# Output projection beside the attention heads, divided anew by columns and tokens, with splits ordered behind evictions

## The chip, the cores and the metric

The kernel runs on one core of one Trainium2 chip. The metric is device microseconds of one execution of the whole layer; lower is better. Five engines work side by side: TensorE (PE in the profile; PEld are its weight loads), VectorE (DVE), ScalarE (ACT), GpSimd (POOL) and SyncE (SP), which issues nearly all DMAs here. Each engine runs its instructions in order and waits for the others through semaphores.

## The reference

One layer on x of 1024 tokens by 1024 features, with a memory of 256 tokens, all float32:

```python
h = h + parallel_mixer(rms_norm(h, norm_mix_g), w_in, ..., w_out)
h = h + memory_cross_attention(rms_norm(h, norm_xattn_g), rms_norm(mem, norm_mem_g), ...)
u = jax.nn.relu(rms_norm(h, norm_mlp_g) @ mlp_w1)
h = h + (u * u) @ mlp_w2
```

The mixer projects x, runs forgetting attention over 8 heads of width 64 (causal, softmax of `q.k / 8` plus a sum of log forget gates) and gated linear attention (GLA) over 4 heads, and multiplies both results, side by side, by `w_out`:

```python
return jnp.concatenate([fox_out, gla_out], axis=-1) @ w_out
```

So rows 0 to 511 of `w_out` meet the attention's output and rows 512 to 1023 that of the GLA. The cross attention has 4 heads of width 256 and takes its keys and values from `memn @ wkv`.

## The kernel before

**Products.** Every float32 operand is split into a high part of a shorter format and a low part (the rest), and `gemm` (line 103) makes three matmuls for each k-tile of 128: high by high, high by low, low by high (lines 108 to 110). A split is a copy on ScalarE and a subtraction on VectorE. For weights `wsplit` (line 67) does it: it loads two k-tiles of 128x512 in one DMA on SP into one of 2 `raw` buffers (line 78), copies each to `wh` on ScalarE (line 86) and subtracts to `wl` on GpSimd in two halves (line 89) or on VectorE (line 91). With `lo_pool=1` every tile is subtracted on GpSimd, with 2 every other one, with 0 none. There are 9 slots for `wh` and 9 for `wl`, taken in turn. For the mixer's outputs `split_half` (line 794) splits, for one half of the tokens (512), one k-tile after the other into buffers `sh` and `sl` (lines 802 and 803).

**The heads.** `fox` (line 645) runs 8 heads. A head has two groups of four score blocks and four blocks of values; after each of the 32 value blocks `step(s)` (line 687), s = 0 to 31, advances a generator of side work by one item or by none. Score blocks go from TensorE (`s`, lines 627 to 630) over a maximum on VectorE (632), an exponential on ScalarE (635) and a scaling on GpSimd (638); value blocks transpose p on TensorE (667), split it (115 and 116) and multiply (674 and 675). The result lands in `mixf` (line 680), k-tile h // 2 for head h, so the first two k-tiles of the attention are complete after head 3, the third after head 5. The GLA's output `mixg` is complete before the heads start.

**The side work** (`side_work`, line 704) has 26 items:

- `out_part(.., 0, ())`, items 1 to 8: columns 0 to 511 of the projection, GLA part only. The k-tiles of the GLA are 4, so an item, one block of 128 columns for one half of the tokens, is 4 x 3 = 12 matmuls. First four items for the first half of the tokens, then four for the second.
- items 9 and 10: the memory is loaded and split; the gains `gx` are made (lines 713 to 716).
- items 11 to 18: the keys and values of the memory, `wkv` in four column groups n of 8 k-tiles for two token tiles each: 24 matmuls an item. Results go into one buffer `mkv` and from there by DMA to DRAM (lines 738 and 752).
- `out_part(.., 1, range(2))`, items 19 to 26: columns 512 to 1023, 4 k-tiles of the GLA and 2 of the attention: 18 matmuls an item.

An item of `out_part` ends by adding the residual from x to the accumulator on VectorE (the eviction, line 776, tile `t2k`) and storing the sum in DRAM (`hpd`). The accumulators of the side work come from a pool with one bank (`mm2`, line 650), so the next item's first matmul waits for this one's eviction. Item 1 runs before head 0, and the pacing `(s * 30 + 8) // 32` makes item 26 fall to step 26.

**The projection behind the heads** (`project_out`, line 808) adds what is left: for columns 0 to 511 all four k-tiles of the attention, for columns 512 to 1023 the last two (`ks`, line 815), for both halves of the tokens, with six accumulator banks. It loads `hpd` (line 821), adds it (826), squares the result on ScalarE and adds the squares up on GpSimd (`add_squares`, line 159) for the norm of the cross attention, which follows with its query products.

**Order.** The program states the operations, but the order of instructions on each engine is made by a planner that simulates the whole program in time: an operation may be placed ahead of others of its engine that come earlier in the text, where buffers and data allow. `tc.issue_after(ins)` makes all instructions traced inside it follow `ins` on the engine of `ins`.

Of the kernel before, what the change touches and what calls it, by code (L numbers as in the profile page):

```python
# [22 lines left out]
ALU = mybir.AluOpType  # L23
# [28 lines left out]
class Layer:  # L52
# [59 lines left out]
    def evac_split(self, hi, lo, ps, scale=None):  # L112
        nc = self.nc
        if scale is None:
            nc.scalar.activation(hi, ps, AF.Copy)
            nc.vector.tensor_tensor(lo, ps, f(hi), ALU.subtract)
        else:
            nc.scalar.activation(hi, ps, AF.Identity, scale=scale)
            nc.vector.scalar_tensor_tensor(lo, ps, scale, f(hi), ALU.mult, ALU.subtract)
# [75 lines left out]
    def build(self):  # L195
        with ExitStack() as st:
# [13 lines left out]
            self.consts(self.open(st, "const"))  # L210
            self.smallp = self.open(st, "small", 6)
# [433 lines left out]
    def fox(self):  # L645
        nc = self.nc
        with ExitStack() as st:
# [39 lines left out]
            def step(s):  # L687
                for _ in range(((s + 1) * 30 + 8) // 32 - (s * 30 + 8) // 32):
                    next(side, None)
# [14 lines left out]
    def side_work(self, mp, mmp, trp):  # L704
# [4 lines left out]
        yield from self.out_part(mp, mmp, 0, ())  # L709

        mh, ml = ([self.T(mp, [P, 4, P], F32R, n, bufs=6) for _ in range(4)] for n in ("sh", "sl"))
        gm = self.cols[:, C_MEM:C_MEM + 8]
# [3 lines left out]
        nc.vector.scalar_tensor_tensor(self.gx, self.gx, 0.0625, gk, ALU.mult, ALU.mult)  # L716
        for t in range(2):
# [12 lines left out]
        for n in range(4):  # L730
            W = self.wsplit(self.wkv[:, n * 512:(n + 1) * 512], None, lo_pool=2)
            for t in range(2):
                ps = self.T(mmp, [P, 512], F32, "mm")
                self.gemm(ps, *([m[k // 2][:, 2 * (k % 2) + t, :] for k in range(KT)] for m in (mh, ml)), *W)
                kv = self.T(mp, [P, 2, 512], F32R, "mkv")
                if n >= 2:
                    self.evac_split(kv[:, 0, :], kv[:, 1, :], ps, self.mr[:, t:t + 1])
                    nc.sync.dma_start(self.vmd[:, :, t, (n - 2) * 512:(n - 1) * 512], f(kv))
                    yield
                    continue  # L740
# [14 lines left out]
        yield from self.out_part(mp, mmp, 1, range(2))  # L755

    def out_part(self, mp, mmp, n, ks):
# [4 lines left out]
        W = self.wsplit(self.w_out[512:1024, cs], None, lo_pool=1)  # L762
        if ks:
            W = [a + b for a, b in zip(W, self.wsplit(self.w_out[ks[0] * P:(ks[-1] + 1) * P, cs], None, lo_pool=1))]
        for half in range(2):
            A = self.split_half(mp, self.mixg, half, 6, range(4))
            if ks:
                A = [a + b for a, b in zip(A, self.split_half(mp, self.mixf, half, 6, ks))]
            for i in range(4):
                ps = self.T(mmp, [P, 512], F32, "mm")  # L770
                c = slice(i * P, (i + 1) * P)
                self.gemm(ps, *([w[:, c] for w in w_] for w_ in W), *A)
                xt = self.T(mp, [P, 4, P], F32, "t2k", bufs=3)
                nc.sync.dma_start(xt, self.xT[4 * half:4 * half + 4, :, 4 * n + i, :].rearrange("t p s -> p t s"))
                xt = xt.rearrange("p t s -> p (t s)")
                nc.vector.tensor_tensor(xt, ps, xt, ALU.add)
                nc.sync.dma_start(self.hpd[half, 4 * n + i], xt)
                yield
# [29 lines left out]
    def project_out(self):  # L808

        nc = self.nc  # L810
        with ExitStack() as st:
# [3 lines left out]
            ks = range(4), range(2, 4)  # L815
            Ws = [self.wsplit(self.w_out[ks[n][0] * P:512, n * 512:(n + 1) * 512], None, lo_pool=0) for n in range(2)]
            for half in range(2):
                A = self.split_half(self.side, self.mixf, half, 6, range(4))
                for i in range(KT):
                    hr = self.T(xp, [P, 512], F32, "hr")  # L820
# [3 lines left out]
                    self.gemm(ps, *([w[:, c] for w in W] for W in Ws[i // 4]), *(a[ks[i // 4][0]:] for a in A))  # L824
# [490 lines left out]
```

## Time and profile before

| what | us |
|---|---|
| median of three runs (1474.12 to 1475.75) | 1475.63 |
| the profiled execution | 1472.98 |
| its span, first to last instruction | 1471.2 |
| TensorE busy, share of the span | 97% |
| heads, first score matmul to the last value matmul | 317.6 to 577.3 |
| first and last store of `hpd` issued | 346.9 and 551.6 |
| projection behind the heads, first matmul to the first query matmul | 577.3 to 610.5 |

The page of the profile gives busy times of the engines over the span. A busy TensorE is not one at its peak, since matmuls are pipelined. A view by windows gives the same for chosen stretches, with the clock granted to TensorE (1.00 is full speed) and the share and rate of the DMA. The view of waits lists who waited for whom. In the timeline a row has its start, its duration, engine, line, operation, tiles and shape, and in brackets the idle time ahead of it with what ended it.

### The profile page before, as it was taken

Reading aid. Unit: us, or ns where it says so; the run is one execution under the profiler, and the core shown is the slowest. Engines: PE = TensorE matmul, PEld = TensorE weight load, DVE = VectorE, ACT = ScalarE, POOL = GpSimd, SP = SyncE. Lnnn points to the kernel's source line nnn. Section 1 sums busy time; section 2 is a strip of 40 time slices with the busy share of each in tenths; the row PEclk is TensorE's granted clock in tenths of the full one; section 3 lists DMA queues with packets and bytes.
Section 4 is the critical chain, followed back from the end, with each engine's and each line's share of the span. In section 5 each row is a group of like instructions: output and inputs, shape, how many; then the busy total and the mean of one; then the engine's idle time right before and its main releaser. Section 6 shows DMA issues by size and latency. Waiting matters only on the chain.

```text
span 1471.2 us, 19278 instructions
## 1 busy us (share of the span) xinstructions
PE 1431.4 (97%) x7068; PEld 1194.6 (81%) x7068; DVE 934.4 (64%) x1328; ACT 684.3 (47%) x1095; POOL 432.6 (29%) x456
## 2 busy tenths in 40 slices
PE   8998999999998998999999999999999999999998
PEld 6877888887877787888888878887888878888887
DVE  5386422426776677656654885645556968788797
ACT  4463332326775555445442254545445736345230
POOL 2247503324474411621212200000000442433454
PEclk9999999999999999999999999999999999999999
DMA  8425530258677752414375124444445846337353
GB/s 270 127 48 128 143 85 2 72 160 261 182 195 199 197 156 75 144 38 138 115 243 215 43 73 172 172 172 160 169 157 216 304 142 210 127 110 229 111 204 122
DMA packets 129870, 223.94 MB, mean 152 GB/s; under 512 B 8912, under 2 KB 67312, under 8 KB 127216
## 3 DMA queue, kind: packets, MB, share of 16 engines
q1 hardware_dynamic: 129632, 222.45, 47.3%
q8 instruction: 56, 0.92, 0.3%
q10 hardware_dynamic: 144, 0.26, 0.1%
q14 instruction: 38, 0.31, 0.1%
HBM read 150.59 MB, written 72.09 MB: 151 GB/s over the span
## 4 chain that ended last, share of the span: by engine, by line
PE 82%; DMA 7%; DVE 5%; ACT 3%; issue 1%; POOL 1%; SPq 0%; DVEq 0%; ACTq 0%
PE mm L108 14%; PE mm L109 14%; PE mm L110 14%; PE my L109 7%; PE my L110 7%; PE my L108 7%; PE tr L109 3%; PE tr L108 3%; PE tr L110 3%; PE tr L667 1%; DMA raw<-in_xattn_wkv_dram 1%; PE pv L674 1%; PE pv L675 1%; DMA raw<-in_w_in_dram 1%; PE s L627 1%
## 5 line engine op out<-in xcount | busy, mean ns | idle before, releaser
L109 PE MATMUL my<-x,g 128*128 128x512 f32 x464 | 180.6, 389 | 1.3 <-DVE x L1046 1.3
L108 PE MATMUL my<-x,g 128*128 128x512 f32 x464 | 180.6, 390 | 0.9 <-ACT h L1251 0.9
L110 PE MATMUL my<-x,g 128*128 128x512 f32 x464 | 180.5, 389 | 0.0
L109 PE MATMUL mm<-wl,xh 128*128 128x512 f32 x320 | 126.4, 396 | 3.7 <-DVE wl L98 3.7
L108 PE MATMUL mm<-wh,xh 128*128 128x512 f32 x320 | 127.5, 400 | 0.1
L110 PE MATMUL mm<-wh,xl 128*128 128x512 f32 x320 | 126.3, 395 | 0.0
L1045 ACT ACTIVATE g<-s 128x1024 fp32r<-128x1024 f32 (+1 forms) x72 | 68.8, 963 | 104.7 <-PE my L110 35.5
L1046 DVE TENSOR_TENSOR g<-raw,g 128x512 fp32r<-128x512 f32 (+3 forms) x72 | 69.4, 968 | 67.9 <-ACT g L1045 67.8
L1071 POOL TENSOR_TENSOR s<-raw 128x384 f32<-128x384 f32 (+1 forms) x20 | 26.2, 1309 | 284.3 <-issue 217.6
L109 PEld LDWEIGHTS my<-x,g 128*128 128x128 f32 x464 | 87.1, 188 | 19.7 <-DVE x L1046 1.7
L108 PEld LDWEIGHTS my<-x,g 128*128 128x128 f32 x464 | 87.1, 188 | 19.4 <-ACT h L1251 1.4
L1045 ACT ACTIVATE g<-raw 128x512 fp32r<-128x512 f32 (+3 forms) x72 | 55.5, 773 | 99.7 <-DMA raw<-in_mlp_w_dram 39.3
L110 PEld LDWEIGHTS my<-x,g 128*128 128x128 f32 x464 | 87.1, 188 | 18.0
L1046 DVE TENSOR_TENSOR g<-s,g 128x1024 fp32r<-128x1024 f32 (+1 forms) x72 | 88.6, 1234 | 7.2 <-ACT g L1045 7.2
L1213 DVE TENSOR_TENSOR x<-x 128x1024 fp32r<-128x1024 f32 (+1 forms) x64 | 77.7, 1234 | 17.5 <-ACT x L1212 16.9
L638 POOL TENSOR_SCALAR p<-p,rrec 128x128 f32<-128x128 f32 (+3 forms) x64 | 50.5, 792 | 128.6 <-DVE rrec L637 117.5
L108 PE MATMUL mm<-x,g 128*128 128x512 f32 x220 | 85.8, 390 | 0.0
L110 PE MATMUL mm<-x,g 128*128 128x512 f32 x220 | 85.7, 390 | 0.0
L109 PE MATMUL mm<-x,g 128*128 128x512 f32 x220 | 85.6, 389 | 0.0
L108 PE MATMUL tr<-x,g 128*128 128x512 f32 x212 | 82.5, 389 | 0.0
L109 PE MATMUL tr<-x,g 128*128 128x512 f32 x212 | 82.5, 389 | 0.0
L110 PE MATMUL tr<-x,g 128*128 128x512 f32 x212 | 82.5, 389 | 0.0
(319 smaller groups left out, 3779.5 us busy)
## 6 DMA issues: line engine op xcount, KB each, us to landing
ud<-h SPq DMA_DIRECT2D x32, 768.0 KB
x<-ud SPq DMA_DIRECT2D x48, 512.0 KB
raw<-in_mlp_w_dram SPq DMA_DIRECT2D x20, 1024.0 KB
raw<-in_mlp_w_dram SPq DMA_DIRECT2D x16, 768.0 KB
raw<-in_w_in_dram SPq DMA_DIRECT2D x23, 512.0 KB
raw<-in_xattn_wkv_dram SPq DMA_DIRECT2D x16, 512.0 KB
od<-o SPq DMA_DIRECT2D x32, 256.0 KB
ud<-h SPq DMA_DIRECT2D x32, 256.0 KB
```

The source lines that it names most:

```text
L108: mm(ps, lh[k], rh[k], start=start and k == 0, stop=False, **kw)
L109: mm(ps, lh[k], rl[k], start=False, stop=False, **kw)
L110: mm(ps, ll[k], rh[k], start=False, stop=stop and k == n - 1, **kw)
L627: nc.tensor.matmul(ps[:, c], qa[:, ts], ka[:, c], start=True, stop=False)
L638: nc.gpsimd.tensor_scalar(p[:, 0:n], p[:, 0:n], rr, 1.0, ALU.mult, ALU.mult)
L667: nc.tensor.transpose(o, pp[i][:, kb * P:(kb + 1) * P], self.ident)
L674: nc.tensor.matmul(pv, va[:, kb, :], th[:, js], start=kb == 0, stop=False)
L675: nc.tensor.matmul(pv, va[:, kb, :], tl[:, js], start=False, stop=kb == nb - 1)
L1045: self.nc.scalar.activation(hi, src, AF.Copy)
L1046: self.nc.vector.tensor_tensor(lo, src, f(hi), ALU.subtract)
L1071: eng.tensor_tensor(s[:, 0], raw[:, 3], raw[:, 2], ALU.add)
L1213: nc.vector.tensor_tensor(lo, f(lo), f(hi), ALU.subtract)
```

## The change

It alters five things, all around the side work.

1. **Division of the projection.** `FOX_KT = ((0, 2), (2, 3))` says how many k-tiles of the attention are taken into the side work for columns n and half of the tokens. Columns 0 are done half by half: the first half (GLA only) as items 1 to 4, the second half (with 2 k-tiles of the attention) as items 15 to 18, after the memory (5 and 6) and `wkv` (7 to 14). Columns 1 follow as items 19 to 22 (2 k-tiles) and 23 to 26 (3 k-tiles). `project_out` takes the rest: for columns 0 four k-tiles in the first half and two in the second, for columns 1 two and one. The weights of the GLA for columns 0 are loaded and split twice.
2. **Pacing.** Items 2 to 14 are spread over steps 1 to 15 (with steps 0, 5 and 10 free), items 15 to 26 over steps 17 to 30 (with 16, 21, 26 and 31 free).
3. **Order.** The splits of the mixer's output in `out_part` are traced inside `issue_after` of the last eviction of the side work: on VectorE and ScalarE after a `wkv` eviction with n of 2 or 3, on VectorE alone after an eviction of `out_part`, none at the start.
4. **Engines and buffers.** Low parts of the weights in `out_part` go to GpSimd for every other k-tile (`lo_pool=2`) and else to VectorE; `mkv` gets two buffers; `sh` and `sl` seven each in place of six.
5. **Gains.** `gx` is loaded and made ahead of the first item.

```diff
@@ evac_split, build
-            nc.scalar.activation(hi, ps, AF.Copy)
-            nc.vector.tensor_tensor(lo, ps, f(hi), ALU.subtract)
+            a = nc.scalar.activation(hi, ps, AF.Copy)
+            v = nc.vector.tensor_tensor(lo, ps, f(hi), ALU.subtract)
...
+        return a.ins, v.ins
...
+            self.evicted = ()
@@ fox
             def step(s):
-                for _ in range(((s + 1) * 30 + 8) // 32 - (s * 30 + 8) // 32):
+
+                done = lambda s: s * 13 // 16 if s <= 16 else 13 + (s - 16) * 12 // 15
+                for _ in range(done(s + 1) - done(s)):
                     next(side, None)
@@ side_work
-        yield from self.out_part(mp, mmp, 0, ())
-
-        mh, ml = ([self.T(mp, [P, 4, P], F32R, n, bufs=6) for _ in range(4)] for n in ("sh", "sl"))
-        gm = self.cols[:, C_MEM:C_MEM + 8]
         gk = self.T(mp, [P, 256], F32, "gxk")
         nc.sync.dma_start(self.gx, self.xq_g.partition_broadcast(P))
         nc.sync.dma_start(gk, self.xk_g.partition_broadcast(P))
         nc.vector.scalar_tensor_tensor(self.gx, self.gx, 0.0625, gk, ALU.mult, ALU.mult)
+        yield from self.out_part(mp, mmp, 0, (0,))
+
+        mh, ml = ([self.T(mp, [P, 4, P], F32R, n, bufs=7) for _ in range(4)] for n in ("sh", "sl"))
+        gm = self.cols[:, C_MEM:C_MEM + 8]
...
-                kv = self.T(mp, [P, 2, 512], F32R, "mkv")
+                kv = self.T(mp, [P, 2, 512], F32R, "mkv", bufs=2)
                 if n >= 2:
-                    self.evac_split(kv[:, 0, :], kv[:, 1, :], ps, self.mr[:, t:t + 1])
+                    self.evicted = self.evac_split(kv[:, 0, :], kv[:, 1, :], ps, self.mr[:, t:t + 1])
...
-        yield from self.out_part(mp, mmp, 1, range(2))
-
-    def out_part(self, mp, mmp, n, ks):
+        yield from self.out_part(mp, mmp, 0, (1,))
+        yield from self.out_part(mp, mmp, 1, (0, 1))
+
+
+    FOX_KT = ((0, 2), (2, 3))
+
+    def out_part(self, mp, mmp, n, halves):
...
-        W = self.wsplit(self.w_out[512:1024, cs], None, lo_pool=1)
-        if ks:
-            W = [a + b for a, b in zip(W, self.wsplit(self.w_out[ks[0] * P:(ks[-1] + 1) * P, cs], None, lo_pool=1))]
-        for half in range(2):
-            A = self.split_half(mp, self.mixg, half, 6, range(4))
-            if ks:
-                A = [a + b for a, b in zip(A, self.split_half(mp, self.mixf, half, 6, ks))]
+        kt = self.FOX_KT[n]
+        W = self.wsplit(self.w_out[512:1024, cs], None, lo_pool=2)
+        if kt[halves[-1]]:
+            steps = [(k, min(2, kt[halves[-1]] - k)) for k in range(0, kt[halves[-1]], 2)]
+            W = [a + b for a, b in zip(W, self.wsplit(self.w_out[0:512, cs], None, lo_pool=2, steps=steps))]
+        for half in halves:
+            with ExitStack() as behind:
+                for ins in self.evicted:
+                    behind.enter_context(self.tc.issue_after(ins))
+                A = [a + b for a, b in zip(self.split_half(mp, self.mixg, half, 7, range(4)),
+                                           self.split_half(mp, self.mixf, half, 7, range(kt[half])))]
             for i in range(4):
...
-                self.gemm(ps, *([w[:, c] for w in w_] for w_ in W), *A)
+                self.gemm(ps, *([w[:, c] for w in w_[:4 + kt[half]]] for w_ in W), *A)
...
-                nc.vector.tensor_tensor(xt, ps, xt, ALU.add)
+                self.evicted = nc.vector.tensor_tensor(xt, ps, xt, ALU.add).ins,
@@ project_out
-            ks = range(4), range(2, 4)
-            Ws = [self.wsplit(self.w_out[ks[n][0] * P:512, n * 512:(n + 1) * 512], None, lo_pool=0) for n in range(2)]
+            Ws = [self.wsplit(self.w_out[min(kt) * P:512, n * 512:(n + 1) * 512], None, lo_pool=0) for n, kt in enumerate(self.FOX_KT)]
             for half in range(2):
-                A = self.split_half(self.side, self.mixf, half, 6, range(4))
+                A = self.split_half(self.side, self.mixf, half, 7, range(4))
                 for i in range(KT):
+                    kt = self.FOX_KT[i // 4]
...
-                    self.gemm(ps, *([w[:, c] for w in W] for W in Ws[i // 4]), *(a[ks[i // 4][0]:] for a in A))
+                    self.gemm(ps, *([w[:, c] for w in W[kt[half] - min(kt):]] for W in Ws[i // 4]), *(a[kt[half]:] for a in A))
```

More of the change, by code (lines that the diff above doesn't have):

```diff
@@ L114, in evac_split @@
         if scale is None:
-            nc.scalar.activation(hi, ps, AF.Copy)
-            nc.vector.tensor_tensor(lo, ps, f(hi), ALU.subtract)
-        else:
-            nc.scalar.activation(hi, ps, AF.Identity, scale=scale)
-            nc.vector.scalar_tensor_tensor(lo, ps, scale, f(hi), ALU.mult, ALU.subtract)
+            a = nc.scalar.activation(hi, ps, AF.Copy)
+            v = nc.vector.tensor_tensor(lo, ps, f(hi), ALU.subtract)
+        else:
+            a = nc.scalar.activation(hi, ps, AF.Identity, scale=scale)
+            v = nc.vector.scalar_tensor_tensor(lo, ps, scale, f(hi), ALU.mult, ALU.subtract)
+        return a.ins, v.ins
     def rstd(self, out, ss, inv_n, eps=EPS):
```

## The prediction

> **What bounds the kernel now.** I read the page first, then TensorE's busy time by windows over the fox stage and the output projection, then TensorE's waits, the chain of waits and the timeline at each longer gap.
>
> ```profile
> span 1471.2 us, 19278 instructions
> PE 1431.4 (97%) x7068; PEld 1194.6 (81%) x7068; DVE 934.4 (64%) x1328; ACT 684.3 (47%) x1095; POOL 432.6 (29%) x456
> PE 82%; DMA 7%; DVE 5%; ACT 3%; issue 1%; POOL 1%; SPq 0%; DVEq 0%; ACTq 0%
> 300.00:578.00 278.00, 259.40 (x1500) 219.16 (x1499) 182.52 (x340) 168.52 (x354) 106.03 (x135) 0.97 0.64 182
> 577.28:610.20 32.92, 32.92 (x149) 27.24 (x148) 19.62 (x26) 13.25 (x22) 14.98 (x13) 1.00 0.46 135
> ```
>
> TensorE is busy for 97% of the span and is most of the chain. In a window row the numbers are the width, then the busy time of PE, PEld, DVE, ACT and POOL, the granted clock and the DMA. The fox stage (to 578) leaves TensorE idle for 278.00 - 259.40 = 18.6 us and loses 3% of the clock; the projection behind it (577.28 to 610.2) is full. So a matmul that moves from the projection into the heads is worth its time only if it falls into those 18.6 us, and the rest of the change is worth what it takes out of them. They lie in a few places:
>
> ```profile
> 339.00:349.00 10.00, 7.54 (x28) 5.44 (x26) 8.10 (x16) 5.07 (x12) 6.34 (x7) 0.84 0.96 307
> 450.00:460.00 10.00, 7.51 (x36) 6.59 (x37) 6.07 (x14) 7.11 (x16) 2.74 (x4) 0.66 0.37 99
> 490.00:500.00 10.00, 7.50 (x33) 6.34 (x34) 6.97 (x13) 6.34 (x14) 5.90 (x8) 0.83 0.48 159
> 500.00:540.00 40.00, 40.00 (x237) 34.27 (x236) 27.03 (x50) 20.95 (x44) 6.47 (x8) 1.00 0.71 204
> 551.00:578.00 27.00, 21.40 (x150) 18.70 (x150) 23.75 (x47) 20.24 (x43) 5.97 (x8) 0.94 0.16 49
> PE tr L667 <- DVE mkv L116: 4.2, 1, 4.2
> PE mm L108 <- DVE mkv L119: 3.6, 2, 3.2
> PE mm L108 <- DVE t2k L776: 2.7, 2, 2.5
> ```
>
> Where side blocks simply follow each other (500 to 540) nothing is idle. Each gap also costs clock, taken as width times what is missing of 1.00.
> - **339 to 349**: 2.5 us idle and 0.16 x 10 = 1.6 of clock: 4.1.
> - **448 to 460**: 4.2 idle (the wait row) and 3.4 of clock: 7.6.
> - **489 to 500**: 3.2 idle and 1.7 of clock: 4.9.
> - **551 to 578**, heads with no side work left: 5.6 idle and 0.06 x 27 = 1.6 of clock: 7.2.
>
> Together 23.8 us. The first three have these causes:
>
> ```profile
> 336.78 3.64 DVE L803 TENSOR_TENSOR sl<-mixg,sh 128x512 fp32r<-128x512 f32 x5
> 343.75 0.68 DVE L776 TENSOR_TENSOR t2k<-mm,t2k 128x512 f32<-128x512 f32 x1
> 344.48 0.50 PE L108 MATMUL mm<-sh,wh 128*128 128x512 f32 x1 [2.46 <-DVE t2k L776]
> ...
> 451.11 0.60 ACT L115 ACTIVATE mkv<-tr 128x512 fp32r<-128x512 f32 x1 [4.76 <-DMA kTd<-mkv]
> 452.49 1.11 PE L667 MATMUL tr<-ident,p 128*128 128x128 f32 x4 [4.22 <-DVE mkv L116]
> ...
> 489.44 2.34 DVE L803 TENSOR_TENSOR sl<-mixf,sh 128x512 fp32r<-128x512 f32 x2
> 491.70 0.74 DVE L119 SCALAR_TENSOR_TENSOR mkv<-mm,mr,mkv 128x512 fp32r<-128x512 f32 x1
> 492.50 0.68 PE L108 MATMUL mm<-sh,wh 128*128 128x512 f32 x1 [3.18 <-DVE mkv L119]
> ```
>
> The side work has a single accumulator bank, so its next gemm waits for the eviction (L776, L119). At 343 and 491 that eviction stood on VectorE behind splits (L803) of the coming block. At 451 the one mkv buffer was still being stored, and the copy into it held ScalarE's queue.
>
> **The change part by part.** Durations are of this one execution, 1472.98 us with a span of 1471.2; the median of the runs is 1475.63, 2.65 higher, and I put the difference I find onto the median.
>
> *Matmuls moved.* The spacing of matmuls in a full stretch is the difference of two starts six matmuls apart:
>
> ```profile
> 582.07 0.39 PE L108 MATMUL mm<-sh,wh 128*128 128x512 f32 x1
> 583.43 0.39 PE L108 MATMUL mm<-sh,wh 128*128 128x512 f32 x1
> ```
>
> (583.43 - 582.07) / 6 = 0.227 us. The projection ran 8 x 12 + 8 x 6 = 144 matmuls and will run 4 x (12 + 6 + 6 + 3) = 108: 36 fewer, 8.2 us off. The side work ran 8 x 12 + 8 x 18 = 240 beside the memory and will run 4 x (12 + 18 + 18 + 21) = 276: 36 more, 8.2 us on. The sum of TensorE's work is zero; what counts is idle time and clock alone. The new pacing puts the last four blocks (4 x 21 x 0.227 = 19.1 us of matmuls) into head 6's end and head 7, where the trace has 5.6 us idle and no side work. That removes the 7.2 us there, if the seam behind it stays covered (below).
>
> *mkv with two buffers.* The store at 451 no longer blocks: 7.6 us go. What is late next is the load of the wkv weights, which the chain and ScalarE's waits show:
>
> ```profile
> 410.06 7.96 DMA raw<-in_xattn_wkv_dram
> 423.84 3.73 DMA raw<-in_xattn_wkv_dram
> 430.27 4.91 DMA raw<-in_xattn_wkv_dram
> ACT wh L86 <- DMA raw<-in_xattn_wkv_dram: 15.4, 7, 6.2
> ```
>
> The bounds of that are 0 (matmuls of the heads fill the time) and the 7.6 gained; I give back 2.5, nearer nothing, since the new pacing also stretches the eight wkv items from eight steps to nine.
>
> *Splits behind evictions, gx early, first block of one half.* No second half's splits and no gx product stand before the evictions at 343, and at 491 the eviction goes first: 4.1 + 4.9 go. But the wait is added elsewhere: at the three later block starts (columns 0 half 1, columns 1 half 0 and half 1) six or seven splits now queue behind the eviction on VectorE, and the block's matmuls behind them; on ScalarE only the copies after a wkv eviction do. Prices:
>
> ```profile
> L802 ACT ACTIVATE sh<-mixg 128x512 fp32r<-128x512 f32 x16 | 9.3, 624 | 0.3
> L803 DVE TENSOR_TENSOR sl<-mixg,sh 128x512 fp32r<-128x512 f32 x16 | 11.5, 753 | 5.0 <-ACT sh L802 4.9
> L86 ACT ACTIVATE wh<-raw 128x512 fp32r<-128x512 f32 x47 | 28.2, 629 | 24.7 <-DMA raw<-in_xattn_wkv_dram 15.4 <-DMA raw<-in_w_out_dram 7.9 <-PE mm L109 1.2
> L91 DVE TENSOR_TENSOR wl<-raw,wh 128x512 fp32r<-128x512 f32 x22 | 18.4, 840 | 7.8 <-ACT wh L86 7.6 <-PE mm L109 0.2
> L89 POOL TENSOR_TENSOR wl<-raw,wh 128x256 fp32r<-128x256 f32 x50 | 42.1, 865 | 27.6 <-ACT wh L86 27.6
> ```
>
> At least the first pair, 0.62 + 0.69, has to end before the first matmul: 1.3 us a start, after which a k-tile takes TensorE 3 x 0.227 = 0.68 and VectorE 0.75. Bounds are 0 (fox matmuls stand between) and the 4.9 of the gap at 489. I take 1.3 at each of three, 4.0.
>
> *More operands.* The weight tiles split in the side work go from 4 + 6 to 4 + 6 + 7, the splits of the attention from 8 + 12 to 4 + 6 + 6 + 7. ScalarE gets 10 x 0.63 = 6.3 us more. Low parts of weights on POOL go from 10 tiles to 9, on VectorE from none to 8; with three more L803 VectorE gets 8 x 0.84 + 3 x 0.75 = 9.0 us more in the heads, to 191.5 of 278. Nine weight loads instead of five are issued on SP, 7 x 0.26 = 1.8 MB more, at 182 GB/s some 10 us of transfer, asked for from step 15 on, with steps free of side work (16, 21) ahead of the gemms. VectorE is not the bound from 500 to 540 (27.03 of 40 beside a full TensorE). Bounds 0 and 9.0; I take 1.5.
>
> *The seam.* This is the last eviction of the present side work:
>
> ```profile
> 550.88 0.68 DVE L776 TENSOR_TENSOR t2k<-mm,t2k 128x512 f32<-128x512 f32 x1
> ```
>
> Side work ended at 551.6, and splits for the projection and the queries ran while the heads finished. After the change the last block holds seven of nine weight slots and all seven split buffers until its last gemm, so four weight tiles and four splits of the first half come after it: 8 x (0.75 to 0.84) = 6.4 us on VectorE. They can begin as that gemm passes each k-tile (4.8 us long), and head 7's last matmuls lie behind. Bounds 0 and 6.4 + 1.7 of clock; I take 4.0 (2.3 idle and 1.7 of clock). The second half of the projection shrinks to 36 x 0.227 = 8.2 us, while POOL needs seven adds for its squares:
>
> ```profile
> L167 POOL TENSOR_TENSOR acc<-acc,sqT 128x512 f32<-128x512 f32 x14 | 20.3, 1450 | 23.3 <-ACT sqT L166 22.5
> ```
>
> 7 x 1.45 = 10.2 us; the 2.0 over are covered by the first two query gemms (48 x 0.227 = 10.9), which need only the first half's norm. Without that cover they cost 2.0.
>
> Sum: -23.8 + 2.5 + 4.0 + 1.5 + 4.0 = -11.8 us. Against the execution 1461.2, against the median 1463.8: **1464**.
>
> ```profile
> PE pv L675 <- DVE ptl L116: 1.8, 1, 1.8
> ```
>
> On the clock, the trace first: after the 2.46 us gap at 344 and this one of 1.8 us near 553 the granted clock falls (0.84 and 0.94 in the window rows). The Trainium skill, "TensorE: Matmul & The Clock Gate", section "Why this matters for your kernels", says that only idle gaps above about 3 us send the clock back to half. This trace disagrees, and the measurement decides; by the rule the seam's gap would cost no clock, and the sum would be 1.7 us lower.
>
> **The rivals.**
> - *All cover holds.* The new waits fall under fox matmuls, as the 500 to 540 window suggests; only some 4 of the 12 us are paid: -20, 1456.
> - *The weight loads take the place of the mkv wait.* Three wkv loads on the chain above speak for it, a mean DMA share of 0.64 against. The 7.6 us come back: -11.8 + 7.6 - 2.5 = -6.7, 1469.
> - *The change doesn't do what it says.* The order on each engine is planned for the whole program; other operations could move into the freed places. Half of the gains with all new costs leave -11.9 + 12.0 = +0.1: 1476.
> - *Slower: splits exposed behind the evictions.* Place: the three block starts and the seam. Speaking for it: the 489 gap shows such a start uncovered, 4.9 us; and from 551 VectorE is busy 23.75 of 27 us while TensorE idles. Price: 3 x 4.9 + 8.1 at the seam = 22.8 in place of my 8.0, with VectorE's 9.0 counted in full, because those ops are the splits, in place of 1.5: -23.8 + 2.5 + 22.8 + 9.0 = +10.5; with half of VectorE's, +6: 1482. It decides once new waits pass 23.8 + 3 = 27 us. Against it: idle steps stand before two of the starts, and at the start of the second half near 520 the present kernel idles nowhere.
>
> **How the numbers follow.** Forecast (1459 to 1468) 0.50; all cover holds 0.16; late weight loads 0.14; not what it says 0.08; exposed splits 0.12. About 3 us (0.2%) is what a measurement of this kernel can tell from no change, so faster means below 1472.7. Faster: 0.50 + 0.16 + 0.11 of the late loads = 0.77; same: 0.03 + 0.08 = 0.11; slower 0.12. The range from 1454 to 1477 leaves out the exposed splits and a little at the lower end.
>
> **What would show it.** Right: no wait on mkv near 450; no L108 wait on t2k near 343; the projection some 24.6 us long and full; the projection starting near 574 (578 - 23.8 + 8.2 + 12.0) in place of 577.3, and TensorE over 25 us busy in the last 27 of the heads. Wrong: L108 waiting at the block starts for sl or wl, TensorE idle over 5 us between the last pv matmul and the projection, or L86 waiting for wkv loads by more than 15.4 us.

## The result, and the profile after

The changed kernel takes 1483.37 us (median; the kernel before beside it 1472.43): ratio 1.0067, interval 1.0049 to 1.0085, so some 10 us **slower**. The forecast was 1464 and the range ended at 1477. One execution of the changed kernel took 2893 us, one of raw3_before 2895 and one of half4_after 2033; the ratios leave these out. The profiled execution took 1483.22 us, its span is 1481.5. First the page of the changed kernel: span, busy times and the engines' shares of the chain.

```profile
span 1481.5 us, 19293 instructions
PE 1436.8 (97%) x7068; PEld 1195.2 (81%) x7068; DVE 942.5 (64%) x1339; ACT 688.5 (46%) x1105; POOL 434.0 (29%) x454
PE 81%; DMA 9%; DVE 5%; ACT 2%; issue 1%; POOL 1%; SPq 0%; DVEq 0%; ACTq 0%; POOLq 0%
```

TensorE's instructions are as many as before. DMA on the chain went from 7% to 9%. To see where the 10.3 us of the spans arise, I take three marks from the timelines of both kernels: the last write of `mixf` in head 3 and in head 7, and the first matmul of the query products. First the kernel before, then the changed one.

```profile
461.66 0.42 DVE L680 TENSOR_TENSOR mixf<-pv,ol 64x256 f32<-64x256 f32 x1
...
577.90 0.42 DVE L680 TENSOR_TENSOR mixf<-pv,ol 64x256 f32<-64x256 f32 x1
...
610.45 0.39 PE L108 MATMUL mm<-wh,sh 128*128 128x512 f32 x1
```

```profile
466.66 0.42 DVE L682 TENSOR_TENSOR mixf<-pv,ol 64x256 f32<-64x256 f32 x1 [0.24 <-ACT ol L679]
...
590.48 0.42 DVE L682 TENSOR_TENSOR mixf<-pv,ol 64x256 f32<-64x256 f32 x1
...
616.78 0.75 PE L108 MATMUL mm<-wh,sh 128*128 128x512 f32 x1 [2.36 <-ACT sqT L167]
```

| stretch, us | before | after | difference |
|---|---|---|---|
| to the end of head 3 | 461.66 | 466.66 | +5.0 |
| heads 4 to 7 (8.2 of matmuls moved in) | 116.24 | 123.82 | +7.6 |
| heads' end to first query matmul (8.2 moved out) | 32.55 | 26.30 | -6.3 |
| from there to the end of the span | 860.75 | 864.72 | +4.0 |

No stretch behaves as forecast. The first four heads should have won the gaps at 344 and 452; they lost 5. Heads 4 to 7 should have taken the moved matmuls into idle time; they pay for nearly all. The projection gives back less than was taken out, and what follows it is longer.

The waits of the changed kernel from 300 to 650 (microseconds, times, longest), then SP's own waits at the loads of raw weights, before and after:

```profile
PE s L629 <- ACT p L637: 6.3, 4, 2.8
PE tr L669 <- POOL p L640: 4.4, 3, 2.3
PE mm L108 <- ACT sqT L167: 2.4, 1, 2.4
PE mm L109 <- DVE sl L815: 1.3, 3, 0.8
PE mm L108 <- DVE t2k L788: 1.3, 1, 1.3
ACT wh L86 <- DMA raw<-in_xattn_wkv_dram: 21.2, 8, 6.8
```

```profile
SPq L78 <- DVE wl L91: 46.7, 13, 11.7
SPq L78 <- POOL wl L89: 6.6, 8, 1.9
```

```profile
SPq L78 <- DVE wl L91: 55.8, 20, 7.1
SPq L78 <- POOL wl L89: 5.0, 7, 1.6
```

The gaps that were to go are gone or smaller: no wait on `mkv`, 1.3 us for `t2k`. Others stand in their place, and they are mostly no longer at the side work's gemms but at the heads' own scores (L629) and transposes (L669). Over the heads (from 300 to the last write of `mixf`) TensorE is idle for 20.2 us; before it was 18.6. ScalarE stands 21.2 us, not 15.4, at the copy of a `wkv` weight (L86). And the row that the prediction never asked for: SP stands 55.8 us at the issue of a weight load, because the raw buffer it needs is still being read by a subtraction (L91). One such case from the changed kernel's timeline, with rows of all engines (start, duration, engine, line):

```profile
380.56 0.68 DVE L91 TENSOR_TENSOR wl<-raw,wh 128x512 fp32r<-128x512 f32 x1
381.86 0.40 SPq L78 DMA_DIRECT2D raw<-in_xattn_wkv_dram  x1
...
385.83 1.42 POOL L89 TENSOR_TENSOR wl<-raw,wh 128x256 fp32r<-128x256 f32 x2
387.28 0.40 SPq L78 DMA_DIRECT2D raw<-in_xattn_wkv_dram  x1
...
389.73 1.15 ACT L86 ACTIVATE wh<-raw 128x512 fp32r<-128x512 f32 x2 [5.28 <-DMA raw<-in_xattn_wkv_dram]
390.79 0.77 ACT L637 ACTIVATE p<-s,nm 128x640 f32<-128x640 f32 x1
391.70 0.51 PE L629 MATMUL s<-ka,qa 128*128 128x512 f32 x1 [1.68 <-ACT p L637]
```

The chain of waits over the same stretch has the load between two of these rows:

```profile
381.86 7.79 DMA raw<-in_xattn_wkv_dram
```

Read it downwards. VectorE's subtraction ends at 381.24 and a buffer is free; SP issues the next load at 381.86. It takes 7.79 us, and until 389.73 ScalarE stands 5.28 us at the copy that needs it, with the next exponential queued behind. That comes at 390.79, and TensorE has waited 1.68 us for it. The second buffer is no help: GpSimd's subtraction holds it until 387.25, and its load goes out at 387.28. "ACT p", which TensorE's row names, is the last of four steps.

### The profile page after: what moved, and what is told of

The parts are those of the page before. It is cut to its first block, busy times and chain, and to the rows that moved or that the text cites. A ratio compares the mean times of both kernels' runs of the same rounds, so it can differ in the third digit from the quotient of the medians.

```text
span 1481.5 us, 19293 instructions
## 1 busy us (share of the span) xinstructions
PE 1436.8 (97%) x7068; PEld 1195.2 (81%) x7068; DVE 942.5 (64%) x1339; ACT 688.5 (46%) x1105; POOL 434.0 (29%) x454
## 4 chain that ended last, share of the span: by engine, by line
PE 81%; DMA 9%; DVE 5%; ACT 2%; issue 1%; POOL 1%; SPq 0%; DVEq 0%; ACTq 0%; POOLq 0%
PE mm L108 14%; PE mm L109 13%; PE mm L110 13%; PE my L109 7%; PE my L110 7%; PE my L108 7%; PE tr L108 3%; PE tr L110 3%; PE tr L109 3%; DMA raw<-in_xattn_wkv_dram 2%; PE tr L669 1%; DMA ud<-h 1%; PE pv L677 1%; DMA raw<-in_w_out_dram 1%; PE pv L676 1%
## 5 line engine op out<-in xcount | busy, mean ns | idle before, releaser
L108 PE MATMUL mm<-wh,sh 128*128 128x512 f32 x192 | 78.1, 408 | 3.4 <-ACT sqT L167 2.4
```

The costliest lines, as they stand in the source:

```text
L108: mm(ps, lh[k], rh[k], start=start and k == 0, stop=False, **kw)
```

## The experiments

Eighteen kernels besides the changed one; all ratios are to the kernel before on the same chip, with their intervals. "raw" buffers hold two k-tiles of weights (512 KB) on their way.

### Parts of the change, alone

**The second mkv buffer, in the kernel before.**
```diff
-                kv = self.T(mp, [P, 2, 512], F32R, "mkv")
+                kv = self.T(mp, [P, 2, 512], F32R, "mkv", bufs=2)
```


> The kernel before with two mkv buffers and nothing else. Theory A (the 4.2 us wait for the kTd store and 3.4 us of clock behind it were real cost on the path): 7.6 us faster than before, ratio about 0.995, no gap near 450. Theory B (the gap was cover: behind it the wkv weights come late and ScalarE's queue stands at their copies): within 2 us of before, with more L86 waiting for wkv loads than the 15.4 us of before.

Measured 1475.27, ratio 1.0012 (0.9998 to 1.0026): no gain. Its trace has the wait again one item later, at 457, and the cause with it: ScalarE still stands 4.25 us for the store of an `mkv` buffer.

```profile
456.15 0.69 ACT L118 ACTIVATE mkv<-mm,mr 128x512 fp32r<-128x512 f32 x1 [4.25 <-DMA kTd<-mkv]
457.68 0.50 PE L108 MATMUL mm<-wh,sh 128*128 128x512 f32 x1 [3.42 <-DVE mkv L119]
```

So two buffers didn't take the store out of the way, and this run doesn't tell what the gap at 452 was worth. As theory B had it, ScalarE's wait for `wkv` rose, to 18.5 us; but that doesn't show that the gap was cover. The gap at 492 is missing in this trace too, without gain; no weight copy waits for its load there.

**The order behind the evictions, in the kernel before** (`issue_after` as in the change).
```diff
+            with ExitStack() as behind:
+                for ins in self.evicted:
+                    behind.enter_context(self.tc.issue_after(ins))
```


> The kernel before with the splits of out_part ordered behind the last eviction and nothing else. Theory A (the gaps at 343 and 489 were evictions behind splits): both gaps go, 5 to 9 us faster. Theory C (the order exposes the splits at each block start instead): 0 to 8 us slower, with L108 or L109 waiting for sl at the block starts.

Measured 1475.91, ratio 1.0016 (1.0004 to 1.0027): no gain either. In its trace the gap at 492 is gone. The one near 343 is not:

```profile
342.89 0.50 PE L108 MATMUL mm<-sh,wh 128*128 128x512 f32 x1 [2.21 <-DVE t2k L787]
```

VectorE stood there at the product for `gx` (2.53 us for the load of `gxk`), which this run leaves ahead of the eviction. In the kernel before the same product waits 1.05 us, until 341.48, beside the splits that the prediction named.

**The division and pacing alone** (one mkv buffer, no order, old engines).

> The new division by columns and halves with its pacing alone: one mkv buffer, no order behind evictions, low parts of out_part on GpSimd alone, gains made where they were. Theory D (the division carries the loss: the heads take nearly all of the 8.2 us of moved matmuls, the query products start worse, and the wkv stage loses time): 10 us or more slower than before, and slower than the changed kernel if the other parts help. Theory C or B: within 3 us of before.

Measured 1489.88, ratio 1.0115 (1.0095 to 1.0134). The division carries the loss; the other parts of the change win back about 0.5% on top of it, though on the kernel before they win nothing.

**All but the division.**
```diff
-    FOX_KT = ((0, 2), (2, 3))
+    FOX_KT = ((0, 0), (2, 2))
```
with the old order of blocks and the old pacing.

> The old division and the old pacing with all other parts of the change (two mkv buffers, order behind evictions, every other low part on VectorE, gains early, seven split buffers). Theory A with D: 8 to 15 us faster than before. Theory B and C: no faster than before, up to 8 us slower.

Measured 1476.06, ratio 1.0011 (0.9995 to 1.0027): the parts that were to remove three gaps, together, move nothing. Here the causes are gone: no wait of TensorE on `mkv`, and 1.2 us idle near 343 in place of 2.5, now behind an exponential. Other waits have come up, at 364 behind an eviction (2.1 us) and at 497 at a copy of a weight that is late:

```profile
497.31 0.50 PE L108 MATMUL mm<-sh,wh 128*128 128x512 f32 x1 [2.36 <-ACT wh L86]
```

Over its heads TensorE is idle for 20.5 us, no less than the 18.6 of the kernel before.

### The division taken apart

**Order of blocks, pacing and the second weight load, nothing moved** (the changed kernel with `FOX_KT = ((0, 0), (2, 2))`).

> The changed kernel with FOX_KT = ((0, 0), (2, 2)): the new order of the blocks, the new pacing, the second load of the GLA's weights for columns 0 and all else of the change stay, but no matmul of the projection moves into the heads (144 matmuls stay behind them, as before). Theory 1, the 36 moved matmuls are what costs: they are paid in the heads (8.2 us) and not won back in full behind them; then this kernel is near the one with all but the division, 1476 us (ratio 1.000 to 1.003), and its heads end near 583 instead of 590.5. Theory 2, the order and pacing of the blocks with the weights loaded twice costs: 1481 to 1485 (ratio 1.005 to 1.008), whatever is moved, and heads 4 to 7 stay near 124 us less the 8.2 of the matmuls at most in small part.

Measured 1479.08, ratio 1.0039 (1.0024 to 1.0055), between the two theories.

**Only the third k-tile, with the old order of blocks** (all but the division, `FOX_KT = ((0, 0), (2, 3))`).

> The kernel with all but the division, with FOX_KT = ((0, 0), (2, 3)): order of blocks and pacing of the kernel before, and only the third k-tile of the attention for the last four blocks moves into the heads, 12 matmuls, 2.7 us. Theory 1, moved matmuls are paid in the heads and won back behind them only in part (6 of 8.2 in the whole change): 1476 to 1478.5, that is 0 to 2.5 us over the kernel with all but the division (1476.06), ratio 1.001 to 1.004. My prediction's view, that moved matmuls fall into idle time of the heads: 1473.4, ratio 0.998 to 1.000. Theory 2 (order and pacing cost, not the matmuls): 1476, unchanged.

Measured 1481.42, ratio 1.0056 (1.0036 to 1.0077). It moves 2.7 us of matmuls and costs 0.45% or some 5 to 7 us over all but the division (measured on another chip), more than either theory allowed. The windows over the end of the projection and the first queries (width, busy PE, PEld, DVE, ACT, POOL, clock, DMA) show part of it: before, blocks_only, third_tile_only, and the changed kernel.

```profile
600.00:640.00 40.00, 40.00 (x198) 33.53 (x197) 27.42 (x37) 18.03 (x32) 19.02 (x24) 1.00 0.38 119
```
```profile
600.00:640.00 40.00, 40.00 (x192) 33.39 (x191) 25.80 (x34) 18.36 (x31) 22.66 (x25) 1.00 0.43 137
```
```profile
600.00:640.00 40.00, 37.10 (x169) 30.28 (x168) 26.66 (x34) 19.06 (x31) 24.87 (x24) 0.96 0.46 141
```
```profile
600.00:640.00 40.00, 35.53 (x161) 29.05 (x160) 26.97 (x34) 19.10 (x30) 25.97 (x24) 0.96 0.53 165
```

TensorE is full there in the two kernels with nothing moved; in the other two it loses 2.9 and 4.5 us, and 0.04 x 40 = 1.6 us of clock.

**Side work that ends three steps earlier** (the changed kernel).
```diff
-                done = lambda s: s * 13 // 16 if s <= 16 else 13 + (s - 16) * 12 // 15
+                done = lambda s: s * 13 // 16 if s <= 16 else min(13 + (s - 16), 25)
```


> The changed kernel with the second part of the pacing one item a step from step 16 on: items 15 to 26 at steps 16 to 27 instead of 17 to 30. Theory of the seam: the last four blocks reach into head 7's end, so that the splits for the projection and the queries are late and VectorE is the bound from the heads' end to the queries; with the side work ending some 10 us earlier, the heads' end to first query stays under 26 us, the wait at the first query matmul (2.4 us) and the one on L640 at 579 (2.3 us) go, and the time falls by 3 to 5 us, to 1478 to 1480. Theory of the full heads: what is crowded into fewer steps is paid there, and steps without side work are exposed at the end instead, as in the kernel before; then 1483 or slower.

Measured 1488.99, ratio 1.0104 (1.0085 to 1.0124): 5 us slower than the change. The theory of the seam falls. Nor do the waits at the weights explain it: SP's for buffers are 52.8 us (60.8 in the change) and ScalarE's for `wkv` 17.0 (21.2). Over the heads the granted clock is 0.96 in place of 0.98, some 6 us of 298; the cause of that isn't shown.

### The supply of weights

**Three raw buffers in the changed kernel.**
```diff
-            self.rawp = self.open(ws, "raw", 2)
+            self.rawp = self.open(ws, "raw", 3)
```


> The changed kernel with three raw buffers for weights on their way instead of two. Theory of the weight supply: copies on ScalarE (L86) that stand at the head of its queue and wait for a load (21.2 us for wkv alone; at 389 and 511 TensorE then waits for an exponential behind them) set the pace of the heads; with one more load under way those waits fall to under 12 us and the time by 3 us or more, to 1480 or less. Rival: the waits are ScalarE's slack, TensorE's gaps come up elsewhere: within 2 us of 1483.

Measured 1472.66, ratio 0.9991 (0.9978 to 1.0005): some 11 us off the changed kernel (1.0067 to 0.9991) by one buffer; the theory had asked for 3 or more. In its trace, of the longest of its eleven runs (1479.27), ScalarE's wait for `wkv` falls from 21.2 to 7.4:

```profile
ACT wh L86 <- DMA raw<-in_xattn_wkv_dram: 7.4, 3, 4.2
```

**The control: three raw buffers in the kernel before**, nothing else.

> The kernel before with three raw buffers instead of two, nothing else: the control for the gain of three raw buffers in the changed kernel (1483.4 to 1472.7, 10.7 us). Theory W, the division asks for more weights in the heads (GLA weights of columns 0 twice, a seventh k-tile) and two raw buffers can't supply them, while they just suffice for the kernel before: little gain here, 1471 to 1474, ratio 0.998 to 1.000. Rival: weights on their way are short in both kernels, and the third buffer is worth about the same 10 us whatever the division; then 1463 to 1466, ratio 0.993 to 0.995, and the change costs its 10 us on this ground too.

Measured 1465.34, ratio 0.9941 (0.9918 to 0.9964). The rival was right: the supply is short in both kernels. Its waits on SP and ScalarE, and its marks:

```profile
SPq L78 <- POOL wl L89: 16.4, 10, 4.1
SPq L78 <- DVE wl L91: 16.2, 8, 6.0
ACT wh L86 <- DMA raw<-in_xattn_wkv_dram: 10.3, 6, 2.6
```
```profile
569.32 0.42 DVE L680 TENSOR_TENSOR mixf<-pv,ol 64x256 f32<-64x256 f32 x1
...
601.85 0.39 PE L108 MATMUL mm<-wh,sh 128*128 128x512 f32 x1
```

The heads end 8.6 us earlier (577.90 to 569.32). With one mkv buffer and with splits in any order, the gap that I had laid to the splits is gone. The windows around 492, before and with three buffers:

```profile
485.00:500.00 15.00, 11.82 (x66) 10.05 (x65) 8.44 (x14) 9.52 (x19) 9.10 (x12) 0.89 0.57 181
```
```profile
485.00:500.00 15.00, 15.00 (x88) 12.55 (x87) 11.16 (x22) 6.86 (x16) 4.41 (x6) 1.00 0.77 229
```

The splits (L803, 480.16 to 482.44) still stand right ahead of the eviction there (L119, 482.36). What differs is ScalarE. In the kernel before, a copy of a weight waited 3.33 us for its load, and the copies that those splits need were queued behind it; with three buffers no weight copy waits there ahead of them:

```profile
486.82 1.15 ACT L86 ACTIVATE wh<-raw 128x512 fp32r<-128x512 f32 x2 [3.33 <-DMA raw<-in_w_out_dram]
```

The other three places that the prediction counted are still there with three buffers: the gap behind `t2k` near 344, the store of the one `mkv` buffer in ScalarE's way (TensorE then waits 2.57 us at 444.96 for the exponential behind it), and the heads' end:

```profile
PE mm L108 <- DVE t2k L776: 2.4, 2, 2.2
```
```profile
443.22 0.60 ACT L115 ACTIVATE mkv<-tr 128x512 fp32r<-128x512 f32 x1 [3.26 <-DMA kTd<-mkv]
```
```profile
540.00:570.00 30.00, 24.55 (x157) 21.60 (x156) 25.02 (x49) 20.43 (x45) 5.98 (x8) 0.89 0.16 47
```

**Three raw buffers with nothing moved, and with 24 matmuls moved.** raw3_blocks is blocks_only with three buffers. no_third is the changed kernel with `FOX_KT = ((0, 2), (2, 2))`, raw3_no_third the same with three buffers.

> The changed kernel with three raw buffers and FOX_KT = ((0, 0), (2, 2)): the new order of blocks and pacing with the weights supplied, no matmul moved. Theory W: the 4.8 us that blocks_only loses come from the weights loaded twice through two buffers, so 1470 to 1474 here, ratio 0.997 to 1.000. If moved matmuls do fall into idle time of the heads once the weights are there, raw3_no_third is faster than this one by 3 us or more; if they are paid in the heads, the two are equal or this one is faster.

> The changed kernel with FOX_KT = ((0, 2), (2, 2)): 24 matmuls moved into the heads instead of 36, and the last four blocks of the projection keep 6 matmuls each (1.36 us) instead of 3 (0.68 us). Theory T, the projection's tail: with 3 matmuls a block VectorE's evictions, with the splits for the queries between them, and the sums of squares on POOL are the bound; at 610 to 640 the changed kernel lost 2.4 + 2.1 us idle and 1.6 us of clock, blocks_only with 12 and 6 nothing. Then this kernel is 4 to 6 us faster than the changed one: 1477.5 to 1479.5, ratio 1.002 to 1.004, and TensorE is full from 600 to 640. Rival, all moved matmuls cost alike: a third of the 4.3 us between blocks_only and the changed kernel, 1.4 us: 1482.

> no_third with three raw buffers. If the weight supply and the tail are separate costs they add up: 1472.7 - 4 to 6 = 1467 to 1469, ratio 0.995 to 0.997, faster than both kernels. If the tail's wait only came up behind the other (no sum), 1471 to 1474.

| moved into the heads | two raw buffers | three raw buffers |
|---|---|---|
| kernel before | 1 | 0.9941 (0.9918 to 0.9964) |
| new order and weights twice, none | 1.0039 (1.0024 to 1.0055) | 0.9946 (0.9932 to 0.9960) |
| 24 matmuls | 1.0078 (1.0058 to 1.0098) | 0.9958 (0.9942 to 0.9975) |
| 36 matmuls, the change | 1.0067 (1.0049 to 1.0085) | 0.9991 (0.9978 to 1.0005) |

With two buffers the new order and the first 24 matmuls cost 0.4% each and the last 12 nothing that can be told; leaving out the third k-tile didn't help, and theory T missed by 8 us there. With three, the new order and the second load of weights cost nothing that can be told, the first 24 matmuls 0.1%, within the intervals, and the last 12 another 0.3% or 5 to 6 us, the size that T had. T's sign isn't there, though: in raw3_no_third TensorE is busy for 37.25 of the 40 us from 600 to 640, at a clock of 0.96. The loss of the change over the kernel before is then 0.9991 - 0.9941 = 0.5%, and it lies mostly in the third k-tile.

**Four half buffers: the same memory, one k-tile a load.** In the kernel before and in the changed one:
```diff
-            raw = self.T(self.rawp, [P, 2, N], F32, "raw")
...
             for j in range(n):
+                raw = self.T(self.rawp, [P, 1, N], F32, "raw")
+                self.raw_load = eng.dma_start(raw[:, 0], src[(k0 + j) * P:(k0 + j + 1) * P, :])
```


> The kernel before with the weights loaded one k-tile at a time into four raw buffers of half the size: the same bytes under way and the same memory as two buffers of two k-tiles, but each buffer is free, and its next load issued, after one subtraction instead of two. Theory F, the time until a buffer comes free sets the pace (SP waits at the raw loads for L91 46.7 us and for L89 6.6): a good part of the 9.4 us of the third buffer comes without any more memory, 1466 to 1470, ratio 0.994 to 0.997. Theory B, the bytes under way set it: 1473 to 1476, or slower by the doubled number of loads on SP.

> The changed kernel with the same four half buffers. Theory F: 1473 to 1478, that is 5 to 10 us under the changed kernel's 1483.4, ratio 0.999 to 1.002. Theory B: 1482 to 1485, ratio 1.005 to 1.007.

The kernel before: 1472.63, ratio 0.9980 (0.9963 to 0.9998). The changed one: 1475.40, ratio 0.9999 (0.9983 to 1.0015). In the changed kernel buffers that come free one k-tile sooner bring 0.7% of the 0.8% that a third buffer brings; in the kernel before only 0.2% of 0.6%. That theory B (the bytes under way) has the rest there isn't shown: in the trace of half4_before ScalarE stands 5.3 us for the store of the one `mkv` buffer, which the changed kernel has twice. SP's and ScalarE's waits of half4_after:

```profile
SPq L79 <- DVE wl L91: 22.6, 17, 3.6
SPq L79 <- POOL wl L89: 11.0, 14, 1.7
ACT wh L86 <- DMA raw<-in_xattn_wkv_dram: 7.4, 3, 4.5
```

SP's wait for buffers, over the heads, fell from 60.8 (55.8 + 5.0) to 33.6 us, and ScalarE's for `wkv` to 7.4 as with three buffers.

**Buffers freed by GpSimd instead of VectorE**, in the kernel before (`lo_pool=1` for `wkv`).

> The kernel before with all low parts of wkv on GpSimd (16 tiles more there, 2 x 0.865 us each, 27.7 us; 16 x 0.84 = 13.4 us less on VectorE). If raw buffers come free late because VectorE stands behind the heads' work, GpSimd (106 of 278 us busy in the heads) frees them sooner: 1466 to 1470, ratio 0.994 to 0.997. If GpSimd's two halves of 0.87 us, behind the scaling of p, are slower than that, or it then delays the scaling that the transposes wait for: 1475 to 1482, ratio 1.000 to 1.005.

Measured 1481.69, ratio 1.0056 (1.0038 to 1.0074). The buffers don't come free sooner: SP waits 30.4 us for GpSimd, 21.3 for ScalarE's copies and 2.6 for VectorE, 54.3 in sum, where the kernel before has 6.6, 1.9 and 46.7, 55.2 in sum. The transposes don't wait longer for the scaling of p either (0.6 us, before 1.3), but the scores wait 7.1 us for exponentials (before 1.3).

### The tail of the projection

**Six buffers for the loads of hpd**, on top of three raw buffers, in the changed kernel.
```diff
-                    hr = self.T(xp, [P, 512], F32, "hr")
+                    hr = self.T(xp, [P, 512], F32, "hr", bufs=6)
```


> The changed kernel with three raw buffers (1472.7) and six buffers for hr in the projection behind the heads instead of three. If the loads of hr (256 KB a block, for blocks of 0.68 us of matmuls) bound the tail that the third k-tile makes: 4 to 6 us less, 1467 to 1469, ratio 0.995 to 0.997, as without the third k-tile. If VectorE's evictions behind the query splits and the squares on GpSimd bound it: 1471 to 1474, unchanged.

Measured 1471.29, ratio 0.9966 (0.9950 to 0.9981), against 0.9991 (0.9978 to 1.0005) with three: 0.25%, of which the intervals leave little certain. The ratio lies in the range of the loads of `hr`, the time in that of the evictions and squares, so the two aren't told apart. Its trace over the last of the projection, and its marks:

```profile
600.00:610.00 10.00, 8.53 (x40) 6.90 (x39) 9.88 (x11) 6.40 (x11) 9.69 (x6) 1.00 0.30 100
```
```profile
577.58 0.42 DVE L682 TENSOR_TENSOR mixf<-pv,ol 64x256 f32<-64x256 f32 x1 [2.02 <-ACT ol L679]
...
605.23 0.47 PE L108 MATMUL mm<-wh,sh 128*128 128x512 f32 x1 [1.47 <-DVE h L838]
```

With the loads there, VectorE is busy 9.88 and GpSimd 9.69 of 10 us while TensorE is busy 8.53. That makes them the likely bound of blocks of three matmuls (3 x 0.227 = 0.68 us against an eviction of 0.68, the query splits between, and 1.4 for a sum of squares on GpSimd).

**Both supplies mended, with and without the change**, on one chip.

> The kernel before with three raw buffers and six for hr in the projection. If hr loads cost only where blocks are short (after matmuls were moved): as with three raw buffers alone, ratio 0.993 to 0.995, 1465 to 1468. If they also hold the projection of the kernel before (VectorE waited 8.0 us for hr with three raw buffers, but TensorE was full from 600 to 640): 2 us less, ratio 0.991 to 0.993.

> no_third (24 matmuls moved, 5.4 us) with three raw buffers and six for hr. If moved matmuls fall into idle time of the heads once both supplies are mended, it is under raw3_hr6_before by 2 us or more. If they are paid in the heads and won back behind them, the two are equal within 2 us; if the projection still gives back less than what was moved, this one is 2 to 5 us slower, ratio 0.995 to 0.998.

Measured 1464.64, ratio 0.9940 (0.9918 to 0.9961), without the change, and 1467.50, ratio 0.9951 (0.9932 to 0.9970), with it and 24 matmuls moved. The intervals overlap; the medians are 2.9 us apart in favour of nothing moved. Neither is there a sign that moved matmuls pay. With six `hr` buffers the third k-tile costs 0.15% (0.9951 to 0.9966), within the intervals. The best kernels of the study are thus the kernel before with three raw buffers, with or without six for `hr`: some 9 us faster than before, 18 faster than the change.

## Why the prediction was wrong

**The gaps, -23.8.** This step failed. It priced each gap at its length plus lost clock, by its last releaser, and took that as won once the releaser was gone. all_but_division took the releasers of the gaps at 452 and 492 away and halved the gap at 344, and gained nothing (1.0011): other waits came up, and TensorE's idle time over the heads was 20.5 us, before 18.6. In the changed kernel it was 20.2, where the forecast would have taken 15.5 of the 18.6 away. Of the two single tests, order_only removed one gap of its two without gain, and mkv2_only left its own cause standing. For the gap at 492 the runs show what was behind the releaser: a weight that came late held ScalarE's queue. Where no weight is late there (mkv2_only and three raw buffers), the gap is gone with the splits still ahead of the eviction. The gap at 344, the store of `mkv` and the idle end of the heads were not of that kind: they stay with three raw buffers. At the heads' end the change won little: in their last 27 us TensorE is busy for 23.5, before 21.4, at a clock of 0.94 in both; the forecast asked for over 25.

**The loads of wkv, +2.5.** The right mechanism, in the prediction's rivals too, and mis-sized. I bounded it by the 7.6 us of the mkv wait, from the view of ScalarE's waits and the mean DMA share of 0.64. A mean share under 1 says only that the DMA engines have time, not that a load is asked for in time: SP's view of its own queue had 46.7 + 6.6 us of waiting at the raw loads. The chain of one load above shows both halves of it: 7.79 us under way, and the other buffer held meanwhile. Measured, a third buffer is worth 9 us in the kernel before and 11 in the changed one. The prediction's own sign of being wrong, L86 waiting for `wkv` by more than 15.4 us, came true (21.2).

**Matmuls moved, zero in sum.** Half wrong. With three raw buffers, the heads end at 569.32 (raw3_before) or 570.29 (raw3_blocks) with nothing moved, and at 577.58 with 36 matmuls moved (raw3_hr6): 7.3 to 8.3 us for 8.2 moved. TensorE's idle time over the heads is 13.8 us in raw3_before and 13.0 in raw3_hr6, so the matmuls are paid nearly in full and don't go into idle time. These are single traces; in that of raw3_after, the longest of its runs, the heads end at 584.22. That alone would be near the zero sum. But behind the heads the change gives back less: the first query matmul follows the heads' end by 32.53 us in raw3_before, 34.14 in raw3_blocks and 27.65 in raw3_hr6, 4.9 to 6.5 instead of 8.2.

**The projection's second half, "covered by the first two query gemms".** Wrong, and the cover was gone twice. VectorE's evictions stood behind the query splits, in the changed kernel's timeline:

```profile
612.53 2.62 DVE L802 TENSOR_TENSOR sl<-h,sh 128x1024 fp32r<-128x1024 f32 x2 [0.57 <-issue]
615.27 1.36 DVE L838 TENSOR_TENSOR h<-mm,hr 128x512 f32<-128x512 f32 x2
```

and the first query matmul waited 2.36 us (its row stands above). Its weights were late on ScalarE as well, where their copies (L97) shared the queue with copies of h (L801) and squares (L167):

```profile
616.75 0.27 PEld L108 LDWEIGHTS mm<-wh,sh 128*128 128x128 f32 x1 [2.57 <-ACT wh L97]
```

And everything from the first query matmul on takes 864.7 us in place of 860.8. The spans less that mark give 859.7 to 861.6 in the ten kernels with nothing moved into the heads (the kernel before among them) and 862.6 to 867.4 in the ten with matmuls moved. Some 4 us are lost there, and I had counted nothing.

**Block starts, +4.0, and extra operations, +1.5.** The waits were small: 1.3 us for `sl` in three places, of which 0.8 at 342, in the first block, where none was forecast, and 0.5 at the first of the three forecast starts. VectorE in the heads wasn't measured alone.

**The seam, +4.0.** The right place: TensorE waited 2.3 us at 579 for the scaling of p. But the test that ended the side work earlier made the kernel slower, so the seam isn't what decides.

**The slower rival** gave 1482 and the kernel takes 1483, but by another mechanism: exposed splits cost 1.3 us of waits, not 14.7. A right number from a wrong cause: luck.

**What stays open.** Why TensorE's idle time comes up again in all_but_division, beyond the one late weight shown. Why leaving the third k-tile out loses with two raw buffers (1.0078 against 1.0067) and wins with three. And what all of the some 4 us behind the first query matmul are made of. A part can be seen: in five of the ten kernels with moved matmuls TensorE waits 2.6 to 3.2 us at the first transposes of the queries (L980), in none of the other ten; the profile puts that wait down to nothing that it shows.

## What to carry to other kernels

A gap is worth its length only if nothing else is late behind it, and a test of its cause counts only if its trace shows the cause gone: before pricing its last releaser, look into the DMA queue's own waits for loads that stand for a buffer to come free, and try one more buffer first. Work that moves out of a short stage takes cover away from what runs beside it: count the other engines' time for each block that gets shorter (here 0.68 us of matmuls against 0.68 of eviction and 1.4 of squares). And idle time in a stage isn't room for more work: 36 more matmuls left the heads as idle as they were, with two raw buffers (18.6 and 20.2 us) and with three (13.8 and 13.0).

## What the runs showed of the hardware

The granted clock after a gap isn't told by the gap's length alone. In raw3_no_third a gap of 2.75 us stands in a window with the clock at 0.83, in raw3_hr6 one of 2.64 us at the same instruction in windows at 1.00:

```profile
610.00:620.00 10.00, 7.25 (x30) 5.74 (x29) 7.10 (x10) 2.14 (x3) 5.08 (x8) 0.83 0.61 190
```
```profile
610.00:620.00 10.00, 7.36 (x38) 6.01 (x37) 4.56 (x7) 3.20 (x4) 6.03 (x8) 1.00 0.25 71
620.00:640.00 20.00, 20.00 (x105) 17.15 (x105) 10.56 (x16) 6.70 (x15) 7.09 (x13) 1.00 0.26 91
```

The prediction charged clock for every gap; here one of two costs none. The Trainium skill, "TensorE: Matmul & The Clock Gate", section "Why this matters for your kernels", puts the limit for the clock at idle gaps of about 3 us; the second row would agree, the first (0.83 after 2.75 us) does not. A limit between 2.64 and 2.75 us would fit these two, but not the rest: the gap of 2.36 us at 616.78 in the changed kernel stands in a window with the clock at 0.84 (610 to 620), and one of 1.8 us near 553 in the kernel before lost clock too (0.50 from 555 to 557). No single length fits.
